# A hybrid decoder trunk: one weight combination of the Strassen MLP made by adding DMAs in place of VectorE, with the first two blocks' sums loaded ahead

## The chip, the cores and the metric

The kernel runs on one core of a Trainium2 chip. A core has four engines that compute: TensorE (PE, matmuls), VectorE (DVE), ScalarE (ACT) and GpSimd (POOL). SyncE (SP) issues transfers. Each engine works through its own list of instructions in order. The metric is the device time of one execution in microseconds; lower is better.

## The reference

The input is 512 tokens of width 1024 in float32. Two layers follow one another; each adds a mixer and then an MLP to the residual stream, and a final norm ends it.

```python
for i in range(DEPTH):                         # DEPTH = 2
    xn = rms_norm(x, norm_mix[i])
    mix = mla_mixer(xn, ...) if i % 2 == 0 else gla_mixer(xn, ...)
    x = x + mix
    x = x + sq_relu_mlp(rms_norm(x, norm_mlp[i]), mlp_w_up[i], mlp_w_down[i])
return rms_norm(x, final_norm)

def sq_relu_mlp(xn, w_up, w_down):             # w_up 1024 x 4096, w_down 4096 x 1024
    return jnp.square(jax.nn.relu(xn @ w_up)) @ w_down
```

The change lies in the two MLPs, in the norm that prepares their input, and in one small instruction at the start.

## The kernel before

**Precision.** A float32 matrix product is made of three products of the type fp32r. Each operand is split into a high part (ACT copies it into fp32r, line L112) and a low part (VectorE subtracts the high part from the value, L115). TensorE adds high by high, high by low and low by high. In the MLPs all weight pieces are split on the way in by `piece`, which names the parts `wh` and `wl` (three buffers each). Every matmul of an MLP is on line L818 (`matmuls`); it multiplies a 128x128 weight piece with 128x256 of the tokens.

**Strassen.** An MLP's products are made by the Winograd form of Strassen's scheme: seven block products in place of eight. In the up projection there are eight blocks b of 512 output columns. The 1024x512 weights of a block are cut into four quarters of 512x256, named 11, 12, 21 and 22 (in the code `a11`, `a12`, `a21`, `a22`, each 128x1024 in SBUF, 512 KB). The tokens are cut likewise; their combinations T1 to T4 are made once per MLP by `combine`. The seven steps of `up_block`, in the order in which the first two blocks run them:

- s0 and s1 load the quarters and multiply 11 by x11.
- s2 multiplies 12 (the product called "21").
- s5 makes S = 21 + 22 on VectorE (L904) and multiplies it by T1.
- s6 makes S - 11 (L919) and multiplies it by T2.
- s3 makes 12 - S (L925), multiplies it by x22 (the product "22"), and adds what belongs to it out of PSUM (L928).
- s7 makes 11 - 21 on VectorE (L932) and multiplies it by T3; L935 takes the sum out of PSUM.
- s4 multiplies 22 by T4, into the PSUM bank that L935 has read.

`finish` (L862, L863) applies relu, the norm's factor and the square. From block 2 on, s5 stands ahead of s2, there is no s0, and the steps alternate with those of a down projection.

The down projection works on pairs of blocks: `down_block(s)` for s = 0, 1, 2, with seven steps p1, p5, p6, p7, p2, p3, p4 on quarters of 512x512 (128x2048 in SBUF, 1 MB). p7 makes 11 - 21 of the weights on VectorE (L1004). The hidden values' combinations are on VectorE too (the `b11`, `b12`, `b21`, `b22` lines). Blocks 6 and 7 go through a plain product (`down`, `down_final`).

**Loads and buffers.** SP loads up quarters into five buffers of 512 KB (pool `up`, tag `raw`) and down quarters into three of 1 MB (pool `down_w`, tag `raw`). For blocks 0 and 1 the quarters 21 and 22 come as one 1 MB load each into a buffer of the down weights (`wide[b]`, L1116), because the up buffers still hold other data at that time. The third of these buffers takes the first down quarter, which is loaded directly behind (L950).

**Order.** A scheduler places the instructions of each engine; `tc.keep_in_program_order` holds some where they are written, `tc.issue_after` holds a load behind another.

## Time and profile before

| | us |
|---|---|
| median of three runs | 1080.58 |
| the runs | 1080.05, 1080.58, 1083.18 |
| the profiled execution | 1080.79 |
| its span in the trace | 1079.1 |

The profile is of one execution; 1.7 us of its time lie outside the span. Its page gives the busy time of each engine, a chain of work that ended last, and groups of instructions. The mean clock granted to TensorE was 0.997 of full speed. In the rows of the trace, a line's start and length are in microseconds, "x2" counts instructions that a row joins, and a bracket behind a row is the idle time ahead of it with what ended it. The products of the first MLP begin between 190 and 195 us, those of the second between 740 and 745.

### The profile page before, as it was taken

What the parts mean: (1) busy time and instruction counts of PE and PEld (TensorE: products, weight loads), DVE (VectorE), ACT (ScalarE), POOL (GpSimd) and SP (SyncE); (2) the same over time, 40 slices, a digit from 0 to 9 for tenths busy, and PEclk for the clock granted to TensorE, in tenths of its full rate; (3) what the DMA queues carried; (4) which work ended last, traced back from release to release, by engine and by line L of the source; (5) the groups of instructions that cost most, each with busy time, mean ns of one, the idle gap of its engine ahead of it and who ended that gap; (6) DMA issues with size and microseconds to landing.
All of it is one profiled execution on the core that took longest, in us unless ns stands there. A gap on an engine that the chain in (4) does not pass through costs nothing.

```text
span 1079.1 us, 17824 instructions
## 1 busy us (share of the span) xinstructions
PE 1058.9 (98%) x7322; PEld 977.1 (91%) x7322; DVE 890.0 (82%) x1210; ACT 640.2 (59%) x934; POOL 44.5 (4%) x78
## 2 busy tenths in 40 slices
PE   9999999989999999999999999999899999999997
PEld 7788888989999999988788888888899999999986
DVE  6789879999899899967565655678999899899865
ACT  6577655566667776644334735655565667766734
POOL 6400000000000000030000000000000000000000
PEclk9999999999999999999999999999999999999999
DMA  7312017143433433260222222234324423522412
GB/s 211 95 49 79 13 31 229 42 136 99 157 98 99 157 100 96 86 203 24 62 67 78 79 79 57 61 98 138 117 79 129 146 82 134 176 76 82 137 39 79
DMA packets 97969, 107.88 MB, mean 100 GB/s; under 512 B 8048, under 2 KB 72832, under 8 KB 97888
## 3 DMA queue, kind: packets, MB, share of 16 engines
q1 hardware_dynamic: 95872, 105.52, 31.1%
q8 instruction: 57, 0.93, 0.4%
q10 hardware_dynamic: 1952, 1.21, 0.4%
q0 software_dynamic: 64, 0.02, 0.1%
q14 instruction: 24, 0.20, 0.1%
HBM read 104.64 MB, written 2.10 MB: 99 GB/s over the span
## 4 chain that ended last, share of the span: by engine, by line
PE 84%; DVE 11%; issue 2%; ACT 2%; DMA 1%; SPq 0%; DVEq 0%; ACTq 0%
PE ps L818 39%; PE ps L120 12%; PE ps L122 12%; PE ps L121 12%; DVE wl L115 4%; PE ps L137 2%; PE ps L1371 2%; DMA wraw_ckv<-in_mla_w_in_dram 1%; DVE q L862 1%; DVE h L115 1%; DVE raw L925 1%; ACT wh L112 1%; DVE raw L932 1%; DVE raw L904 0%; PE ps L1408 0%
## 5 line engine op out<-in xcount | busy, mean ns | idle before, releaser
L112 ACT ACTIVATE wh<-raw 128x1024 fp32r<-128x1024 f32 x208 | 218.9, 1057 | 155.2 <-PE ps L818 84.3
L115 DVE TENSOR_TENSOR wl<-raw,wh 128x1024 fp32r<-128x1024 f32 x208 | 251.8, 1218 | 16.6 <-ACT wh L112 16.3
L818 PE MATMUL ps<-h,wh 128*128 128x256 f32 x1344 | 170.6, 279 | 0.0
L818 PEld LDWEIGHTS ps<-h,wh 128*128 128x128 f32 x1344 | 163.0, 188 | 0.0
L818 PE MATMUL ps<-h,wl 128*128 128x256 f32 x672 | 92.3, 279 | 2.1 <-DVE wl L115 2.1
L120 PE MATMUL ps<-set,wh 128*128 128x512 f32 x232 | 92.0, 397 | 0.7 <-ACT set L245 0.7
L121 PE MATMUL ps<-set,wh 128*128 128x512 f32 x232 | 91.2, 393 | 0.6 <-DVE set L246 0.6
L122 PE MATMUL ps<-set,wl 128*128 128x512 f32 x232 | 91.1, 393 | 0.0
L112 ACT ACTIVATE wh<-wraw 128x1024 fp32r<-128x1024 f32 x41 | 43.0, 1056 | 74.0 <-PE ps L122 41.5
L818 PEld LDWEIGHTS ps<-h,wl 128*128 128x128 f32 x672 | 84.5, 188 | 2.5 <-DVE wl L115 2.5
L863 ACT ACTIVATE q<-q 128x512 f32<-128x512 f32 x64 | 40.0, 629 | 46.4 <-DVE q L862 46.2
L120 PE MATMUL ps<-wh,set 128*128 128x512 f32 x144 | 59.7, 414 | 0.0
L115 DVE TENSOR_TENSOR wl<-wraw,wh 128x1024 fp32r<-128x1024 f32 x41 | 50.3, 1230 | 10.7 <-ACT wh L112 10.6
L115 DVE TENSOR_TENSOR h<-q,h 128x1024 fp32r<-128x1024 f32 x44 | 53.6, 1220 | 4.9 <-ACT h L112 4.9
L122 PE MATMUL ps<-wh,set 128*128 128x512 f32 x144 | 56.3, 391 | 0.0
L121 PE MATMUL ps<-wl,set 128*128 128x512 f32 x144 | 56.3, 391 | 0.0
L121 PEld LDWEIGHTS ps<-set,wh 128*128 128x128 f32 x232 | 44.0, 190 | 10.5 <-DVE set L246 1.3
L120 PEld LDWEIGHTS ps<-set,wh 128*128 128x128 f32 x232 | 43.9, 190 | 10.0 <-ACT set L245 1.0
L122 PEld LDWEIGHTS ps<-set,wl 128*128 128x128 f32 x232 | 44.0, 190 | 9.0
L112 ACT ACTIVATE h<-q 128x1024 fp32r<-128x1024 f32 x44 | 46.2, 1052 | 4.8 <-DVE q L988 2.1
L818 PE MATMUL ps<-T0h,wh 128*128 128x256 f32 x128 | 33.2, 283 | 7.1 <-DVE q L935 6.7
L120 PE MATMUL ps<-hh,wh 128*128 128x512 f32 x96 | 37.4, 389 | 0.0
(512 smaller groups left out, 2778.2 us busy)
## 6 DMA issues: line engine op xcount, KB each, us to landing
raw<-in_mlp_w_down_dram SPq DMA_DIRECT2D x38, 1024.0 KB, 5.2
raw<-in_mlp_w_up_dram SPq DMA_DIRECT2D x56, 512.0 KB, 3.9
wraw<-in_gla_w_in_dram SPq DMA_DIRECT2D x11, 1024.0 KB, 5.1
wraw<-in_mla_w_o_dram SPq DMA_DIRECT2D x8, 512.0 KB, 4.8
raw<-in_mlp_w_up_dram SPq DMA_DIRECT2D x4, 1024.0 KB, 8.0
wraw<-in_gla_w_o_dram SPq DMA_DIRECT2D x8, 512.0 KB, 4.9
xT<-in_x_dram SPq DMA_DIRECT2D x6, 256.0 KB, 7.5
wraw_qn<-in_mla_w_uq_dram SPq DMA_DIRECT2D x6, 256.0 KB, 3.4
```

The source lines that it names most:

```text
L112: raised.append(order(ACT.activation(hi, src, AF.Copy)))
L115: return lo_eng.tensor_tensor(lo, src, f(hi), ALU.subtract)
L120: PE.matmul(psum, wh, xh, start=start, stop=False, **kw)
L121: PE.matmul(psum, wh, xl, start=False, stop=False, **kw)
L122: PE.matmul(psum, wl, xh, start=False, stop=stop, **kw)
L137: PE.transpose(psum, src, ident[: src.shape[0], : src.shape[0]])
L818: return PE.matmul(p[:, m * TH : (m + 1) * TH], w[i][:, k - k0, m * P : (m + 1) * P], x[k][j], start=start, stop=stop, skip_group_check=True,)
L862: DVE.scalar_tensor_tensor(qs, c, 0.0, r, ALU.max, ALU.mult)
L863: ACT.activation(qs, qs, AF.Square)
L925: DVE.tensor_tensor(v["a12"], v["a12"], v["s"], ALU.subtract)
L932: DVE.tensor_tensor(v["a21"], v["a11"], v["a21"], ALU.subtract)
L1371: PE.matmul(p[:, t * 64 : (t + 1) * 64].rearrange("p (n c) -> p n c", c=m), k[:, sl], later, start=True, stop=True)
```

## The change

In each MLP VectorE no longer makes 11 - 21. A DMA on GpSimd's queue loads quarter 11 once more and adds it onto the buffer of quarter 21 (`accum_op=ALU.add`), which makes 11 + 21. To make the sum fit, the lower rows of the tokens are taken negated: `combine` gets the negated gains for two of its terms (`less`, a 128x16 tile, made once at the start by the new L1582), and further signs change in consequence: sums in place of differences at L919 and L925, the minimum in place of the maximum in `finish` for the second half, and signs of the hidden combinations. The down weights' 11 + 21 is made likewise (a 1 MB addition, L1019). In two places of the down block a scalar-and-tensor instruction takes the place of a plain one, of the same size (L1025, L1055).

For blocks 0 and 1 also S = 21 + 22 is made by a DMA: SP loads 21 into a third buffer, and GpSimd's queue adds 22 onto it. The six loads of 512 KB (two blocks times S's first half, 21 and 22) and the four additions now fill all three buffers of the down weights, so the first down quarter is no longer loaded ahead of them.

```diff
-            DVE.scalar_tensor_tensor(t2, u[:, first], g1, t3, ALU.mult, ALU.add)
+            DVE.scalar_tensor_tensor(t2, u[:, first], l1, t3, ALU.mult, ALU.subtract)
...
+            def fill_sums(s):
+                v["s"] = s
+                fill(s, 1, 0)
+                joint(s, 1, 1)
+                fill(wide[b][0], 1, 0)
+                joint(wide[b][0], 0, 0)
+                fill(wide[b][1], 1, 1)
+
+            def joint(t, half, trail):
+                POOL.dma_start(t, rows(half, trail), accum_op=ALU.add)
...
             def s5():
-                s = v["s"] = up.tile([P, KH, 256], F32, tag="raw", bufs=5, name=uname("raw"))
-                if "a12" not in v:
+                if "s" not in v:
+                    v["s"] = up.tile([P, KH, 256], F32, tag="raw", bufs=5, name=uname("raw"))
                     v["a12"] = unit(0, 1)
-                DVE.tensor_tensor(s, v["a21"], v["a22"], ALU.add)
+                    DVE.tensor_tensor(v["s"], v["a21"], v["a22"], ALU.add)
+                    joint(v["a21"], 0, 0)
+                s = v["s"]
...
             def s6():
-                DVE.tensor_tensor(v["s"], v["s"], v["a11"], ALU.subtract)
+                DVE.tensor_tensor(v["s"], v["s"], v["a11"], ALU.add)
             def s3():
-                DVE.tensor_tensor(v["a12"], v["a12"], v["s"], ALU.subtract)
+                DVE.tensor_tensor(v["a12"], v["a12"], v["s"], ALU.add)
             def s7():
-                DVE.tensor_tensor(v["a21"], v["a11"], v["a21"], ALU.subtract)
...
             def p5():
                 v["21"], v["S"] = quarter(1, 0), quarter(1, 1)
                 DVE.tensor_tensor(v["S"], v["21"], v["S"], ALU.add)
-                DVE.tensor_tensor(b11, b12, b11, ALU.subtract)
+                POOL.dma_start(v["21"], rows(0, 0), accum_op=ALU.add)
+                DVE.tensor_tensor(b11, b11, b12, ALU.subtract)
             def p6():
-                DVE.tensor_tensor(b11, b22, b11, ALU.subtract)
+                DVE.scalar_tensor_tensor(b11, b11, -1.0, b22, ALU.mult, ALU.subtract)
             def p7():
-                DVE.tensor_tensor(v["21"], v["11"], v["21"], ALU.subtract)
             def p4():
-                DVE.tensor_tensor(b21, b21, b11, ALU.subtract)
+                DVE.scalar_tensor_tensor(b21, b11, -1.0, b21, ALU.mult, ALU.subtract)
...
         for b in range(2):
-            t = wide[b] = wide_raw().rearrange("p a (b n) -> p (a b) n", b=2)
-            c0 = b * FB + 256
-            wide["last"] = SP.dma_start(t, w_up[:, c0 : c0 + 256].rearrange("(k p) n -> p k n", p=P))
+            wide[b] = halves(wide_raw())
+        for b, t in enumerate(halves(wide_raw())):
+            fills[b](t)
...
+    DVE.tensor_scalar(less, gains[:, GAIN_COL["mlp"] : GAIN_COL["mlp"] + 16], -1.0, None, ALU.mult)
```

In all 26 VectorE instructions go (16 of L932, 6 of L1004, 4 of L904), one small one comes, and 26 adding DMAs come (20 of 512 KB, 6 of 1 MB). The MLP's lines move down: L818 becomes L825, L862 becomes L889, L904 L931, L919 L948, L925 L954, L928 L957, L935 L963, L950 L981, L852 and L1116 L864.

The order of instructions changes as follows. On VectorE at the start of the first MLP, blocks 0 and 1, before (`raw_2248` and `raw_2250` hold 21 and 22 of the blocks, `raw_2390` and `raw_2548` their S):

```order
L925 TENSOR_TENSOR raw_2146<-raw_2146,raw_2390 128x1024
L904 TENSOR_TENSOR raw_2548<-raw_2250 128x1024
L115 TENSOR_TENSOR wl_2456<-raw_2146,wh_2455 128x1024
L115 TENSOR_TENSOR wl_2488<-raw_2248,wh_2487 128x1024
L932 TENSOR_TENSOR raw_2250<-raw_2156,raw_2250 128x1024
L928 TENSOR_TENSOR q_2253<-ps_2392,mt_2452 128x512
L115 TENSOR_TENSOR wl_2519<-raw_2248,wh_2518 128x1024
L862 SCALAR_TENSOR_TENSOR q_2253<-q_2253,rstd_2327 128x512
L115 TENSOR_TENSOR wl_2552<-raw_2548,wh_2551 128x1024
L935 TENSOR_TENSOR q_2253<-ps_2279,mt_2421 128x512
L919 TENSOR_TENSOR raw_2548<-raw_2548,raw_2156 128x1024
```

and now, in the same place (`raw_2251` holds both S, `raw_2249` 21 and 22 of block 0):

```order
L954 TENSOR_TENSOR raw_2147<-raw_2147,raw_2251 128x1024
L115 TENSOR_TENSOR wl_2433<-raw_2251,wh_2432 128x1024
L115 TENSOR_TENSOR wl_2464<-raw_2147,wh_2463 128x1024
L115 TENSOR_TENSOR wl_2495<-raw_2249,wh_2494 128x1024
L115 TENSOR_TENSOR wl_2526<-raw_2249,wh_2525 128x1024
L957 TENSOR_TENSOR q_2263<-ps_2400,mt_2460 128x512
L115 TENSOR_TENSOR wl_2557<-raw_2251,wh_2556 128x1024
L889 SCALAR_TENSOR_TENSOR q_2263<-q_2263,rstd_2337 128x512
L948 TENSOR_TENSOR raw_2251<-raw_2251,raw_2157 128x1024
L963 TENSOR_TENSOR q_2263<-ps_2289,mt_2429 128x512
L954 TENSOR_TENSOR raw_2159<-raw_2159,raw_2251 128x1024
```

L904 and L932 are gone; block 1's S sum with 11 (L948) now stands ahead of L963, where its counterpart L919 stood behind L935.

On VectorE around the last down block of the first MLP, before (`raw_5150` is the down quarter 12):

```order
L115 TENSOR_TENSOR wl_5121<-raw_4988,wh_5120 128x1024
L925 TENSOR_TENSOR raw_4989<-raw_4989,raw_4988 128x1024
L932 TENSOR_TENSOR raw_4953<-raw_4951,raw_4953 128x1024
L1008 TENSOR_TENSOR xT<-ps_5028,xT 128x4x256
L1009 TENSOR_TENSOR sum_0_2243<-ps_5028,sum_0_2243 128x1024
L862 SCALAR_TENSOR_TENSOR q_4949<-ps_4957,rstd_2327 128x512
L1010 TENSOR_TENSOR xT<-xT,sum_0_2243 128x4x256
L115 TENSOR_TENSOR wl_5158<-raw_5150,wh_5157 128x1024
```

and now:

```order
L115 TENSOR_TENSOR wl_5126<-raw_4993,wh_5125 128x1024
L954 TENSOR_TENSOR raw_4994<-raw_4994,raw_4993 128x1024
L1055 SCALAR_TENSOR_TENSOR q_4041<-q_3615,q_4041 128x1024
L1039 TENSOR_TENSOR xT<-ps_5033,xT 128x4x256
L1040 TENSOR_TENSOR sum_0_2244<-ps_5033,sum_0_2244 128x1024
L889 SCALAR_TENSOR_TENSOR q_4954<-ps_4962,rstd_2337 128x512
L1041 TENSOR_TENSOR xT<-xT,sum_0_2244 128x4x256
L115 TENSOR_TENSOR wl_5163<-raw_5155,wh_5162 128x1024
```

L932's place is taken by L1055, the hidden combination of p4, which stood further on.

On SP at the start of the first MLP, before:

```order
L852 DMA raw_2158<-in_mlp_w_up_dram 128x4x256
L1116 DMA raw_2248<-in_mlp_w_up_dram 128x8x256
L1116 DMA raw_2250<-in_mlp_w_up_dram 128x8x256
L950 DMA raw_2782<-in_mlp_w_down_dram 128x4x512
L852 DMA raw_2710<-in_mlp_w_up_dram 128x4x256
```

and now, on SP,

```order
L864 DMA raw_2159<-in_mlp_w_up_dram 128x4x256
L864 DMA raw_2251<-in_mlp_w_up_dram 128x4x256
L864 DMA raw_2249<-in_mlp_w_up_dram 128x4x256 x2
L864 DMA raw_2251<-in_mlp_w_up_dram 128x4x256
L864 DMA raw_2250<-in_mlp_w_up_dram 128x4x256 x2
L864 DMA raw_2714<-in_mlp_w_up_dram 128x4x256
L864 DMA raw_2716<-in_mlp_w_up_dram 128x4x256
L864 DMA raw_2718<-in_mlp_w_up_dram 128x4x256
L981 DMA raw_2787<-in_mlp_w_down_dram 128x4x512
```

and on POOL, where nothing stood between the first mixer and here:

```order
L878 DMA raw_2251<-in_mlp_w_up_dram 128x4x256
L878 DMA raw_2249<-in_mlp_w_up_dram 128x4x256
L878 DMA raw_2251<-in_mlp_w_up_dram 128x4x256
L878 DMA raw_2250<-in_mlp_w_up_dram 128x4x256
L878 DMA raw_2716<-in_mlp_w_up_dram 128x4x256
L1019 DMA raw_2911<-in_mlp_w_down_dram 128x4x512
```

The first down quarter (L950, now L981) moves behind three up loads. On TensorE the order is the same as before.

## The prediction

> **What bounds the kernel now.** I read the page's busy row first, then its chain, then the table of waits by engine.

> ```profile
> span 1079.1 us, 17824 instructions
> PE 1058.9 (98%) x7322; PEld 977.1 (91%) x7322; DVE 890.0 (82%) x1210; ACT 640.2 (59%) x934; POOL 44.5 (4%) x78
> PE 84%; DVE 11%; issue 2%; ACT 2%; DMA 1%; SPq 0%; DVEq 0%; ACTq 0%
> PE ps L818 <- DVE q L935: 6.7, 4, 2.0
> PE ps L818 <- DVE wl L115: 2.4, 3, 1.1
> PE ps L818 <- ACT wh L112: 1.4, 3, 0.5
> ```

> TensorE is busy for 98% of the span, so an edit that only empties VectorE is worth what TensorE waited for it, and no more. The last three rows (total us, times, longest us) are all of those waits at the MLPs' matmuls: 6.7 + 2.4 + 1.4 = 10.5 us. In the timeline of TensorE they are ten places; the bracket gives the wait and what ended it.

> ```profile
> 209.33 0.39 PE L818 MATMUL ps<-x4h,wh 128*128 128x256 f32 x1 [0.47 <-ACT wh L112]
> 217.02 0.36 PE L818 MATMUL ps<-T0h,wh 128*128 128x256 f32 x1 [1.77 <-DVE q L935]
> 232.66 0.39 PE L818 MATMUL ps<-T0h,wh 128*128 128x256 f32 x1 [1.53 <-DVE q L935]
> 445.84 0.86 PE L818 MATMUL ps<-h,wl 128*128 128x256 f32 x5 [1.07 <-DVE wl L115]
> 759.21 0.38 PE L818 MATMUL ps<-T0h,wh 128*128 128x256 f32 x1 [0.41 <-ACT wh L112]
> 762.69 0.38 PE L818 MATMUL ps<-x4h,wh 128*128 128x256 f32 x1 [0.47 <-ACT wh L112]
> 770.39 0.36 PE L818 MATMUL ps<-T0h,wh 128*128 128x256 f32 x1 [1.97 <-DVE q L935]
> 787.26 0.39 PE L818 MATMUL ps<-T0h,wh 128*128 128x256 f32 x1 [1.40 <-DVE q L935]
> 908.78 0.39 PE L818 MATMUL ps<-T0h,wl 128*128 128x256 f32 x1 [0.26 <-DVE wl L115]
> 1001.40 0.86 PE L818 MATMUL ps<-h,wl 128*128 128x256 f32 x5 [1.06 <-DVE wl L115]
> ```

> Seven of the ten lie in the first two blocks of an MLP (209 to 233, 759 to 788), two at the last down block (445.84, 1001.40), one in a later block. Everywhere else VectorE is nearly full too, yet TensorE does not wait. The windows show it, and one loss of another kind (busy us and count of PE, PEld, DVE, ACT, POOL; then the granted clock, DMA share, GB/s):

> ```profile
> 340.00:360.00 20.00, 20.00 (x176) 20.00 (x175) 19.86 (x20) 13.47 (x17) 0.00 (x0) 1.00 0.23 76
> 771.00:775.00 4.00, 4.00 (x23) 4.00 (x23) 3.25 (x4) 2.64 (x3) 0.00 (x0) 0.57 0.83 273
> 775.00:779.00 4.00, 4.00 (x37) 4.00 (x37) 3.95 (x4) 3.24 (x5) 0.00 (x0) 1.00 0.46 134
> ```

> In the steady stretch VectorE works 19.86 us of 20 and TensorE 20.00: time freed there is worth nothing today. Behind the longest wait (770.39) the clock was granted at 0.57, and 23 matmuls went through in 4 us where 37 go at full clock: (37 - 23) / 37 x 4 = 1.5 us lost. No such row stands behind the 1.77 us wait at 217.02.

> **The change, part by part.**

> *What leaves VectorE.* Groups of VectorE (count | busy us, mean ns of one):

> ```profile
> L932 DVE TENSOR_TENSOR raw<-raw,raw 128x1024 f32<-128x1024 f32 x16 | 19.5, 1219 | 0.1
> L1004 DVE TENSOR_TENSOR raw<-raw,raw 128x2048 f32<-128x2048 f32 x6 | 13.7, 2283 | 0.0
> L904 DVE TENSOR_TENSOR raw<-raw 128x1024 f32<-128x1024 f32 x4 | 4.9, 1219 | 0.0
> ```

> All three go: 26 instructions, 19.5 + 13.7 + 4.9 = 38.1 us. If TensorE waited for VectorE all the time, this would be the gain; the ten rows above cap it at 10.5 + 1.5 = 12.0 us. What is left is to ask, place by place, how much of each wait the freed time reaches.

> *The three waits for the high weight part (1.4 us; 209.33, 759.21, 762.69).* ACT's cast is behind a VectorE sum of the first two blocks: two L904 and two L932 stood among them. With four instructions of about 1.1 us fewer ahead of these casts, nothing of a wait of 0.5 us is left. I take 1.4 of 1.4. What comes next there is the sum L948 (formerly L919), which stands earlier by the same amount.

> *The four waits before T4 (6.7 us).* TensorE's T4 product reuses the bank that L935 empties. VectorE before the first of them, and before the second (with T3's first matmul ahead):

> ```profile
> 212.26 0.28 PE L818 MATMUL ps<-T0h,wh 128*128 128x256 f32 x1
> ...
> 212.72 0.68 DVE L928 TENSOR_TENSOR q<-ps,mt 128x512 f32<-128x512 f32 x1
> 213.32 1.22 DVE L115 TENSOR_TENSOR wl<-raw,wh 128x1024 fp32r<-128x1024 f32 x1
> 214.45 0.69 DVE L862 SCALAR_TENSOR_TENSOR q<-q,rstd 128x512 f32<-128x512 f32 x1
> 215.05 1.22 DVE L115 TENSOR_TENSOR wl<-raw,wh 128x1024 fp32r<-128x1024 f32 x1
> 216.19 0.68 DVE L935 TENSOR_TENSOR q<-ps,mt 128x512 f32<-128x512 f32 x1
> ...
> 224.92 1.22 DVE L932 TENSOR_TENSOR raw<-raw,raw 128x1024 f32<-128x1024 f32 x1
> 229.59 0.69 DVE L928 TENSOR_TENSOR q<-ps,mt 128x512 f32<-128x512 f32 x1
> 231.93 0.68 DVE L935 TENSOR_TENSOR q<-ps,mt 128x512 f32<-128x512 f32 x1
> ```

> Block 0: in the changed order five instructions stand in the same place: L957, L115, L889, L948, L963. They are of the same shapes (the 1.22 us sum L948 where an L115 of 1.22 stood), so the chain from the first of them to T4 stays 217.02 - 212.72 = 4.30 us. L957 needs the bank of "22". That product's last matmul starts one matmul (0.11 us) before T3's first at 212.26, and at 0.28 each it ends at 212.43. L928 started 0.29 us after that, because L932 was still running; without it the chain starts some 0.26 us sooner. The wait becomes 1.5 us in each MLP: 0.27 saved of 1.77, 0.47 of 1.97.

> Block 1: the sum between them is in block 0 only, and L932 (224.92) no longer pushes L928, so L963 is there before T3 ends. T3 ends at 232.66 - 1.53 = 231.13. From there it takes L963's 0.68 us, 0.04 us before and 0.05 to 0.15 behind it (216.19 + 0.68 to 217.02 is 0.15, 231.93 + 0.68 to 232.66 is 0.05): a wait of 0.85 us stays whatever VectorE does. Saved: 0.68 and 0.55. Together 6.7 becomes 4.7 or 4.8: I take 1.9.

> *The waits for the low weight part (2.4 us).* The rows around the last down block of the first MLP, and the sum ahead of the 908.78 wait:

> ```profile
> 415.67 1.23 DVE L115 TENSOR_TENSOR h<-q,h 128x1024 fp32r<-128x1024 f32 x1 [0.64 <-ACT h L112]
> 416.81 0.68 DVE L928 TENSOR_TENSOR q<-ps,mt 128x512 f32<-128x512 f32 x1
> 444.57 2.35 DVE L115 TENSOR_TENSOR wl<-raw,wh 128x1024 fp32r<-128x1024 f32 x2
> 904.64 1.23 DVE L932 TENSOR_TENSOR raw<-raw,raw 128x1024 f32<-128x1024 f32 x1
> ```

> At 908.78 the L932 two rows ahead of the awaited cast goes: 1.23 us against a wait of 0.26. At 445.84 the case is less clear: in the changed order a new L1055 (128x1024, scalar and tensor) stands where an L932 stood, so inside this stretch VectorE has as much as before. But its backlog begins at 416.81, behind rows that L1004 and the 0.64 us idle of the row at 415.67 had made late; those sit more than a microsecond sooner, and VectorE runs without a pause to 444.57. The wait is 1.07. I take all 2.4 as gained; the ends are 0.26 (only 908.78) and 2.4.

> *The clock (1.5 us).* The half-clock stretch came behind a 1.97 us wait and not behind 1.77. The forecast has 1.5 there, below both, so I take the 1.5 us as saved; ends 0 and 1.5. [...]

> *New instructions on VectorE.* L1025 and L1055 as scalar-and-tensor of 128x1024 have no row. 128x512 ones have: 0.69 (214.45) against 0.68 for the plain one (212.72), so I take them equal to those they replace; ends: equal, and 0.02 us more each (under 0.3 us in all). One small 128x16 at the start: between nothing and 0.7 us (a 128x512 at 0.68); I take 0, since it is 1/32 of that. Changed signs and min for max cost nothing: the same instruction in the same place.

> *The accumulating DMAs.* 26 of them, on GpSimd's queue, which had small work only (44.5 us busy in the page); no row of before shows one that adds. The nearest rows (KB, median us from issue to landing), the first issues, and the first cast that needs a sum:

> ```profile
> raw<-in_mlp_w_up_dram SPq DMA_DIRECT2D x56, 512.0 KB, 3.9
> raw<-in_mlp_w_up_dram SPq DMA_DIRECT2D x4, 1024.0 KB, 8.0
> invf<-in_inv_freq_dram POOLq DMA_DIRECT2D x1, 16.0 KB, 6.9
> ...
> 177.35 1.00 SPq L1116 DMA_DIRECT2D raw<-in_mlp_w_up_dram  x2
> 199.46 1.06 ACT L112 ACTIVATE wh<-raw 128x1024 fp32r<-128x1024 f32 x1 [0.48 <-DVE raw L904]
> ```

> Low end: adding costs no more than loading. Two 1 MB loads land in 8.0 us together; six fills and four additions are 5.2 MB, so about 20 us: all done at 197. High end: each addition takes a GpSimd landing and a plain load one after the other, 6.9 + 3.9 = 10.8 us, and they run one by one behind a first fill (177.35 + 3.9 = 181.3): 192, 203, 214, 225. Needed are S of block 0 by 199 (cast at 199.46) and S of block 1 by some 211: the subtraction behind its 1.06 us cast is the L115 at 213.32 in the chain above, ahead of L963. For the T3 weights I estimate 207 and 222, some five us ahead of their products (212.26; 231.13 - 2.9). The low end makes all four; the high end is 3 us late for the two latter. I take the low end's side, nearer to the 512 KB load, 3.9 to 6 us each, at no cost. In later blocks the addition is issued behind the sum S and has 18 to 28 VectorE rows, some 20 us, until its cast; in down blocks 31 rows: either price is covered. The 18 MB more of traffic runs beside a DMA share of 0.23 (steady window). If that cover goes, T3 waits.

> *Fills and the down load.* SP issues six loads of 512 KB for two of 1 MB, and the first down quarter goes behind them and three up loads; it is needed tens of microseconds later. Cost nothing; the cover is the same low DMA share.

> *Sum:* 1.4 + 1.9 + 2.4 + 1.5 = 7.2 us. The profiled execution took 1080.79 us, 1.7 outside its span, 0.2 over the median of the three runs (1080.58). 1080.79 - 7.2 = 1073.6; I say 1073.5.

> **Rivals.**

> *A, slower: the additions come late.* If they pass one at a time at the high price, S of block 1 lands 3 us late; VectorE's in-order queue then holds its cast, L963 behind it, and T4, in both MLPs: 6 us of the 7.2 given back, 1079.5. The kernel gets slower by over 0.3% (3.2 us, about what a measurement can tell) from (7.2 + 3.2) / 2 = 5.2 us late, which is (211 + 5.2 - 181.3) / 3 = 11.6 us each, and each further microsecond per addition costs 6 us: at 13 us, 1088. For it: they share one queue, and 16 KB there took 6.9 us. Against: most of that must be a start-up, which overlaps between queued transfers.

> *B, the freed time is just idle.* Only the waits for the high part go, and the small 0.26: VectorE then waits for TensorE at its in-order reads of banks and arrives at T4 and at the last down block as before. Gain 1.7 to 3: 1078 to 1079. For it: two of the largest waits keep L948 or L1055 in the chain.

> *C, the clock drops again,* or stays as it was: 1075.1, still faster. A drop in the first MLP too: 1076.6. For it: the same kind of wait stays at 1.5 us.

> *D, all ten waits go:* 12.0 us, 1068.8. Against: the evacuation of 0.85 us cannot go.

> **How the numbers follow.** Forecast with or without C (gain 4.5 to 9): 0.55. A gain above 9 (D in part): 0.05. A part of it, 3.3 to 4.5: 0.12. B, or A at about the high price (within 0.3%): 0.16. A beyond that: 0.12. So faster 0.72, same 0.16, slower 0.12. Range: up to 1079.5 (B and the high price of A in), from 1071.0 (the 1.5 us waits down to 0.85 each and some more); below and above are left about 0.05 and 0.13. The forecast's own range is 1071.5 to 1076.5.

> **What the changed profile would show.** Right: three waits for L112 gone; waits for L963 four times, near 1.5 and 0.85 us; no wait for L115 at the last down block; 1.00 clock behind T4 of block 0 in both MLPs; VectorE about 37 us less busy. Wrong: a wait of VectorE or ACT on an addition, with TensorE behind it; 512 KB additions that take over 11 us from issue to landing; or VectorE idle ahead of L963 while TensorE waits.

## The result and the profile after

The changed kernel took 1075.14 us (median of 4, 1073.5 to 1075.3) where the kernel before took 1080.89 on the same chip (median of 4): a ratio of 0.994, with a 95% interval of 0.9922 to 0.9958. In a second set on one chip it was 1074.37 for 1083.26, 0.9919 (0.9904 to 0.9934). Forecast were 1073.5 us, a range of 1071.0 to 1079.5, and faster. The profiled execution took 1075.1 us with a span of 1073.4.

The page's first rows and its DMA issues, and the table of TensorE's waits (total us, times, longest):

```profile
span 1073.4 us, 17924 instructions
PE 1057.3 (98%) x7322; PEld 975.7 (91%) x7322; DVE 858.0 (80%) x1185; ACT 640.5 (60%) x934; POOL 76.1 (7%) x104
raw<-in_mlp_w_up_dram POOLq DMA_DIRECT2D x20, 512.0 KB, 6.4
raw<-in_mlp_w_down_dram POOLq DMA_DIRECT2D x6, 1024.0 KB, 9.2
PE ps L825 <- DVE q L963: 4.8, 4, 1.5
PE ps L120 <- ACT set L245: 1.6, 2, 0.9
PE ps L121 <- DVE set L246: 1.1, 1, 1.1
```

VectorE is 32 us less busy, the span 5.7 us shorter. Of the three rows with 10.5 us at the MLPs' matmuls, one is left with 4.8. The waits for the high and the low part are gone. The four that remain, in TensorE's timeline:

```profile
218.12 0.38 PE L825 MATMUL ps<-T0h,wh 128*128 128x256 f32 x1 [1.50 <-DVE q L963]
233.30 0.39 PE L825 MATMUL ps<-T0h,wh 128*128 128x256 f32 x1 [0.78 <-DVE q L963]
768.62 0.39 PE L825 MATMUL ps<-T0h,wh 128*128 128x256 f32 x1 [1.50 <-DVE q L963]
783.50 0.38 PE L825 MATMUL ps<-T0h,wh 128*128 128x256 f32 x1 [0.99 <-DVE q L963]
```

10.5 - 4.8 = 5.7 us of waits. In the windows (columns as in the prediction), the stretch behind the T4 wait of the second MLP is at full clock now, the steady stretch is unchanged for TensorE, and one at the start is not at full clock:

```profile
340.00:360.00 20.00, 20.00 (x176) 20.00 (x175) 19.51 (x18) 12.86 (x16) 1.28 (x1) 1.00 0.44 113
768.70:772.70 4.00, 4.00 (x35) 4.00 (x36) 3.76 (x5) 2.33 (x4) 0.00 (x0) 1.00 0.53 140
16.00:20.00 4.00, 4.00 (x12) 3.17 (x11) 2.51 (x4) 2.00 (x2) 3.66 (x6) 0.57 0.43 125
```

The kernel before passed that stretch of the start at full clock:

```profile
16.00:20.00 4.00, 4.00 (x19) 3.31 (x18) 2.46 (x4) 2.38 (x3) 3.66 (x7) 1.00 0.40 115
```

Lining up the 7322 matmuls of both traces one by one, the changed kernel is 1.9 us behind at the 58th matmul (19.5 us), and from there to the last waits at 996 us it wins 7.6 us: 5.7 of waits, 1.5 of clock, the rest in steps of 0.1 us. The start took 1.9 of them back, which leaves 5.7.

### The profile page after: what moved, and what is told of

The parts are those of the page before. It is cut to its first block, busy times and chain, and to the rows that moved or that the text cites. A ratio compares the mean times of both kernels' runs of the same rounds, so it can differ in the third digit from the quotient of the medians.

```text
span 1073.4 us, 17924 instructions
## 1 busy us (share of the span) xinstructions
PE 1057.3 (98%) x7322; PEld 975.7 (91%) x7322; DVE 858.0 (80%) x1185; ACT 640.5 (60%) x934; POOL 76.1 (7%) x104
## 5 line engine op out<-in xcount | busy, mean ns | idle before, releaser
L112 ACT ACTIVATE wh<-raw 128x1024 fp32r<-128x1024 f32 x208 | 219.4, 1058 | 152.9 <-PE ps L825 100.0
L115 DVE TENSOR_TENSOR wl<-raw,wh 128x1024 fp32r<-128x1024 f32 x208 | 251.5, 1219 | 26.8 <-ACT wh L112 26.3
L825 PE MATMUL ps<-h,wh 128*128 128x256 f32 x1344 | 170.5, 279 | 0.0
L825 PEld LDWEIGHTS ps<-h,wh 128*128 128x128 f32 x1344 | 162.9, 188 | 0.0
L825 PE MATMUL ps<-h,wl 128*128 128x256 f32 x672 | 92.2, 279 | 0.2
L112 ACT ACTIVATE wh<-wraw 128x1024 fp32r<-128x1024 f32 x41 | 43.0, 1056 | 73.9 <-PE ps L122 41.6
L825 PEld LDWEIGHTS ps<-h,wl 128*128 128x128 f32 x672 | 84.5, 188 | 0.6 <-DVE wl L115 0.6
L878 POOL DMA_DIRECT2D raw<-in_mlp_w_up_dram x20 | 25.8, 1290 | 707.3 <-DVE raw L931 313.9
L890 ACT ACTIVATE q<-q 128x512 f32<-128x512 f32 x64 | 40.2, 628 | 46.7 <-DVE q L889 46.3
L115 DVE TENSOR_TENSOR h<-q,h 128x1024 fp32r<-128x1024 f32 x44 | 53.7, 1222 | 9.9 <-ACT h L112 9.8
L115 DVE TENSOR_TENSOR wl<-wraw,wh 128x1024 fp32r<-128x1024 f32 x41 | 50.2, 1227 | 10.8 <-ACT wh L112 10.7
L112 ACT ACTIVATE h<-q 128x1024 fp32r<-128x1024 f32 x44 | 46.1, 1050 | 0.6 <-DVE q L1020 0.6
L825 PE MATMUL ps<-T0h,wh 128*128 128x256 f32 x128 | 33.0, 281 | 4.8 <-DVE q L963 4.8
## 6 DMA issues: line engine op xcount, KB each, us to landing
raw<-in_mlp_w_down_dram SPq DMA_DIRECT2D x38, 1024.0 KB, 5.2
raw<-in_mlp_w_up_dram SPq DMA_DIRECT2D x68, 512.0 KB, 5.5
wraw<-in_gla_w_in_dram SPq DMA_DIRECT2D x11, 1024.0 KB, 5.1
raw<-in_mlp_w_up_dram POOLq DMA_DIRECT2D x20, 512.0 KB, 6.4
raw<-in_mlp_w_down_dram POOLq DMA_DIRECT2D x6, 1024.0 KB, 9.2
wraw<-in_mla_w_o_dram SPq DMA_DIRECT2D x8, 512.0 KB, 4.8
wraw<-in_gla_w_o_dram SPq DMA_DIRECT2D x8, 512.0 KB, 4.8
```

Source lines behind the costliest of these rows:

```text
L112: raised.append(order(ACT.activation(hi, src, AF.Copy)))
L115: return lo_eng.tensor_tensor(lo, src, f(hi), ALU.subtract)
L825: return PE.matmul(p[:, m * TH : (m + 1) * TH], w[i][:, k - k0, m * P : (m + 1) * P], x[k][j], start=start, stop=stop, skip_group_check=True,)
L878: POOL.dma_start(t, rows(half, trail), accum_op=ALU.add)
L890: ACT.activation(qs, qs, AF.Square)
```

## The experiments

All are written from the changed kernel. "Waits" are TensorE's at the MLPs' matmuls, in us, in the one execution of each kernel that was profiled. Of the half clock it is said where the profile has it at an MLP's matmuls.

| | waits before T4 | for the high part | for the low part | sum |
|---|---|---|---|---|
| before | 6.7 | 1.4 | 2.4 | 10.5 |
| changed | 4.8 | 0 | 0 | 4.8 |
| changed, second profile | 5.0 | 0 | 0 | 5.0 |
| blocks 0, 1 only | 7.1 | 0 | 2.4 | 9.5 |
| blocks 0, 1, 2 only | 5.1 | 0 | 2.7 | 7.8 |
| later blocks only | 7.0 | 1.3 | 0 | 8.3 |
| up weights only | 5.2 | 0 | 3.3 | 8.5 |
| no additions | 5.0 | 0 | 0 | 5.0 |
| sum held behind L963 | 4.7 | 0 | 0 | 4.7 |
| both held behind | 3.1 | 0 | 0 | 3.1 |

The two profiles of the changed kernel differ by 0.2 us, so a difference of that size between kernels says nothing.

**Blocks 0 and 1 only.** From block 2 on and in the down blocks VectorE adds 11 to 21 itself:

```diff
             def s7():
+                if b > 1:
+                    DVE.tensor_tensor(v["a21"], v["a11"], v["a21"], ALU.add)
...
             def p7():
+                DVE.tensor_tensor(v["21"], v["11"], v["21"], ALU.add)
```

(with the additions on GpSimd's queue of these blocks taken out)

> Additions by DMA only in the first two blocks of each MLP; from block 2 on and in the down blocks VectorE adds 11 to 21 itself again (18 of the 26 instructions are back). Theory 1 (what counts are the waits in the first two blocks and, by the freed rows right ahead of them, at three later places): the waits for L112 stay gone, the four waits before T4 stay at 1.5 and 0.85 us, the half-clock stretch behind T4 stays away, but TensorE waits again for the low part at three places, about 2.4 us: some 2.4 us slower than the changed kernel, about 3.5 us faster than before. Rival (VectorE's load as such is what counts, 26 us of it is back): two thirds of the gain goes, 1079 us. Rival 2 (the later additions cost hidden time): as fast as the changed kernel or faster.

Measured: 1080.12 us, ratio 0.998 (0.9971 to 0.9989), 5.0 to 5.8 us slower than the changed kernel where theory 1 had 2.4. The waits for the high part are gone and those for the low part back, as expected; but the waits before T4 of block 1 are 2.05 us, longer than before, and all waits together are 4.7 us longer than in the changed kernel. The timeline of TensorE:

```profile
216.85 0.39 PE L825 MATMUL ps<-T0h,wh 128*128 128x256 f32 x1 [1.50 <-DVE q L964]
232.79 0.39 PE L825 MATMUL ps<-T0h,wh 128*128 128x256 f32 x1 [2.05 <-DVE q L964]
768.85 0.38 PE L825 MATMUL ps<-T0h,wh 128*128 128x256 f32 x1 [1.50 <-DVE q L964]
784.79 0.39 PE L825 MATMUL ps<-T0h,wh 128*128 128x256 f32 x1 [2.05 <-DVE q L964]
```

and VectorE ahead of the second of them (L961 is block 2's sum, back; L956 is the changed kernel's L957):

```profile
227.44 1.22 DVE L961 TENSOR_TENSOR raw<-raw,raw 128x1024 f32<-128x1024 f32 x1
228.57 0.69 DVE L956 TENSOR_TENSOR q<-ps,mt 128x512 f32<-128x512 f32 x1
...
230.91 1.22 DVE L115 TENSOR_TENSOR h<-q,h 128x1024 fp32r<-128x1024 f32 x1
232.05 0.69 DVE L964 TENSOR_TENSOR q<-ps,mt 128x512 f32<-128x512 f32 x1
```

Block 2's sum stands ahead of block 1's chain and pushes the low part of a hidden operand into it. So the two parts of the change are not worth the sum of what each is worth alone. In its total the rival's 1079 us came nearer than theory 1; the places of the waits and the next two runs speak against it.

**Blocks 0, 1 and 2 only** tests that: two VectorE instructions less.

```diff
+                    if b == 2:
                         joint(v["a21"], 0, 0)
...
+                if b > 2:
+                    DVE.tensor_tensor(v["a21"], v["a11"], v["a21"], ALU.add)
```

> Adding DMAs in blocks 0, 1 and 2 only; from block 3 on and in the down blocks VectorE adds. Against the run with the first two blocks only, two VectorE instructions less (block 2's 11 + 21 in each MLP). Theory 1 (the instruction ahead of block 1's L957 is what made T4 of block 1 wait 2.05 us): that wait falls to 0.78 to 0.99 us in both MLPs, 2.1 to 2.5 us less for 2.4 us of VectorE; the 2.4 us of waits for the low part stay. Rival: the wait depends on VectorE's load over the whole stretch and falls by a part only.

1077.98 us in one run. Both waits before T4 of block 1 fell, to 0.99 and 1.00 us: 2.1 us for two instructions of 1.2 us, which is what theory 1 asked for. The low part still cost 2.7 us.

**Later blocks only.** Blocks 0 and 1 as before the change (two 1 MB loads, S and 11 + 21 on VectorE).

```diff
-        for b, t in enumerate(halves(wide_raw())):
-            fills[b](t)
+            wide["last"] = SP.dma_start(joined(t), w_up[:, c0 : c0 + 256]...)
...
             def s7():
+                if b < 2:
+                    DVE.tensor_tensor(v["a21"], v["a11"], v["a21"], ALU.add)
```

> The first two blocks as before (two 1 MB loads, S and 11 + 21 on VectorE), the DMA additions from block 2 on and in the down blocks. Theory 1: only the waits for the low part (2.4 us) go, the waits before T4 and for L112 are back as before (6.7 and 1.4 us), and with them the chance of a half-clock stretch of 1.5 us: 1077 to 1079 us. Rival (load as such): two thirds of the gain stays, 1077 or less, and the T4 waits shrink too. The two rivals and theory 1 differ most in the rows of TensorE's waits, not in the total.

Measured: 1079.57 us, 0.9976 (0.9967 to 0.9984), 0.6 us above the expected band; 2.2 us of waits gone (all of the low part's), the four before T4 at 7.0. The half clock came here behind T4 of the first MLP, behind a wait of 1.77 us (windows of this run):

```profile
219.00:223.00 4.00, 3.89 (x22) 3.92 (x23) 3.96 (x4) 2.40 (x3) 0.00 (x0) 0.63 0.91 312
```

The rival that counts VectorE's load as such loses in both: 28 us of it back (12 sums of 1.22 us and 6 of 2.28) or 10 (8 of 1.22) leave nearly the same time.

**Up weights only.** The six 1 MB additions go back to VectorE, the up ones stay.

```diff
-                POOL.dma_start(v["21"], rows(0, 0), accum_op=ALU.add)
...
             def p7():
+                DVE.tensor_tensor(v["21"], v["11"], v["21"], ALU.add)
```

> Adding DMAs for all up weights; the down weights' 11 + 21 on VectorE again (6 instructions of 2.28 us). The question is what removed the 1.07 us waits for the low part at the last down blocks. As the prediction has it (L1004 made VectorE late ahead of the backlog there): both waits of about 1.07 us are back, the waits before T4 and the 0.26 us one are not; 2.1 us slower than the changed kernel at the same clock. Rival (the up sums counted): the waits stay away and the six instructions cost nothing.

1077.04 us in one run. The waits at the last down blocks are back, and longer than before:

```profile
445.20 1.21 PE L825 MATMUL ps<-h,wl 128*128 128x256 f32 x8 [1.55 <-DVE wl L115]
997.66 1.21 PE L825 MATMUL ps<-h,wl 128*128 128x256 f32 x8 [1.71 <-DVE wl L115]
```

The 0.26 us one is not. So it is taking out the down weights' sum that removed the 1.07 us waits, which the prediction said with less certainty than the rest.

**No additions.** All 26 adding DMAs left out, nothing in their place.

```diff
             def joint(t, half, trail):
-                POOL.dma_start(t, rows(half, trail), accum_op=ALU.add)
+                pass
```

> All adding DMAs left out, with nothing in their place (weights of T3 are 21 alone, S of the first two blocks also). Theory 1 (the additions are hidden everywhere): same time as the changed kernel within 0.5 us, same waits. Rival A (they cost, by contention or late landings): faster by the cost, 1 us or more, with a wait of the changed kernel that is gone here.

1073.79 us, waits of 1.50, 0.99, 1.50, 0.99, as in the second profile of the changed kernel. The additions cost nothing that can be seen in the trace: lined up with the first profile of the changed kernel, the matmuls end 0.2 us earlier (spans 1073.2 and 1073.4, both with a half-clock stretch at the start). The median time is 0.6 to 1.4 us lower, in runs whose mean clock is higher (0.9980 for 0.9974); so the times alone don't rule out a cost of up to about a microsecond.

**Two doses of additions.** First, every addition but three in each MLP made twice, one behind the other:

```diff
                 joint(s, 1, 1)
+                if b == 1:
+                    joint(s, 1, 1)
...
                     joint(v["a21"], 0, 0)
+                    joint(v["a21"], 0, 0)
...
                 POOL.dma_start(v["21"], rows(0, 0), accum_op=ALU.add)
+                POOL.dma_start(v["21"], rows(0, 0), accum_op=ALU.add)
```

> Dose for rival A, inside the slack: in each MLP the addition onto S of block 1, and every later addition (blocks 2 to 7, and the down weights'), is made twice, one behind the other (the weights then hold 11 once too often, or 22 in S). In the changed kernel the addition to S of block 1 lands at 202 us and the cast that needs it runs at 212.9; later additions land after 6 us (512 KB) or 9 us (1 MB). A second one costs about 6 to 8 us more. Theory 1 (additions are hidden with about 10 us to spare): same time within 0.5 us and the same waits. Rival A (they were just in time, or the doubled traffic slows other loads): slower, with new waits for L112 or L115.

1074.63 us, the waits of the changed kernel to the tenth:

```profile
PE ps L825 <- DVE q L966: 4.8, 4, 1.5
```

Then the first blocks' four, twice each:

```diff
             def joint(t, half, trail):
                 POOL.dma_start(t, rows(half, trail), accum_op=ALU.add)
+                if b < 2:
+                    POOL.dma_start(t, rows(half, trail), accum_op=ALU.add)
```

> The dose beyond the slack: all four additions of blocks 0 and 1 are made twice in each MLP (S with 22 twice, T3's weight with 11 twice); the later ones as in the changed kernel. On GpSimd's queue the second waits for the first to land. By 8 us for each second addition, S of block 0 lands near 204 (its cast was at 201), S of block 1 near 215 (cast at 213): waits of 2 to 4 us at T1 and up to 3 us at T4 of block 0 in each MLP, 4 to 14 us slower in all. If the time doesn't move, the additions run far quicker than they land in the changed kernel; if it moves by over 30 us, they pass one at a time at 10 us or more each, as rival A had it.

1078.74 us, with waits that the changed kernel does not have:

```profile
205.87 0.39 PE L825 MATMUL ps<-T0h,wh 128*128 128x256 f32 x1 [0.37 <-ACT wh L112]
209.82 0.39 PE L825 MATMUL ps<-T0h,wh 128*128 128x256 f32 x1 [0.94 <-ACT wh L112]
758.15 0.38 PE L825 MATMUL ps<-T0h,wh 128*128 128x256 f32 x1 [0.80 <-ACT wh L112]
761.82 0.39 PE L825 MATMUL ps<-T0h,wh 128*128 128x256 f32 x1 [0.58 <-ACT wh L112]
```

2.7 us of waits at T1 and T2; lined up with the changed kernel's, its matmuls are 3.4 us behind, less than the 4 to 14 expected, since T4 did not wait for S of block 1, which landed at 212.9, ahead of its cast at 214.69. Nor do the waits at T1 and T2 show what a late addition costs. S of block 0 had landed at 202.2, but its cast stands in this kernel behind another ACT instruction that waits for VectorE:

```profile
204.24 0.63 ACT L892 ACTIVATE q<-q 128x512 f32<-128x512 f32 x1 [3.00 <-DVE q L891]
204.78 1.04 ACT L112 ACTIVATE wh<-raw 128x1024 fp32r<-128x1024 f32 x1
```

In the changed kernel the cast (200.95) stands ahead of that instruction (L890, 205.00). So these waits hold the new order of ACT as well as the landing, which came 1.3 us behind the time of the cast in the changed kernel, and the run doesn't separate the two.

**The sum held behind L963.** The prediction left 1.5 us before T4 of block 0, because block 1's L948 stands ahead of L963.

```diff
+                with tc.issue_after(wide["out"].ins) if b == 1 else nullcontext():
                     DVE.tensor_tensor(v["s"], v["s"], v["a11"], ALU.add)
```

(`wide["out"]` is the instruction of L963 in the block ahead)

> The changed kernel with the sum S + 11 of block 1 (L948, 1.14 us) held behind the read of the T3 sum out of PSUM (L963) of block 0, as it stood in the kernel before. Theory 1: the wait before T4 of block 0 falls from 1.5 to about 0.85 us in both MLPs (L963 cannot start before T3 has ended), 1.2 to 1.3 us faster than the changed kernel, and no new wait at T2 of block 1, which comes 11 us later. Rival B (in-order reads make the wait come back elsewhere): L948 late makes T2 of block 1 wait, and the total does not move.

1073.94 us, 0.9924 (0.9911 to 0.9936), and waits of 4.7 us for 4.8: no gain. Block 0's fell to 0.78, block 1's rose to 1.60 and 1.50: rival B, in small, and at T4 of block 1, not at T2. The scheduler put the low part of p5's hidden operand into the free place, ahead of block 1's L963 (here L964):

```profile
228.53 0.68 DVE L889 SCALAR_TENSOR_TENSOR q<-q,rstd 128x512 f32<-128x512 f32 x1
229.13 1.22 DVE L115 TENSOR_TENSOR h<-q,h 128x1024 fp32r<-128x1024 f32 x1
230.26 0.68 DVE L964 TENSOR_TENSOR q<-ps,mt 128x512 f32<-128x512 f32 x1
```

**Both held behind.** The same, and that low part too:

```diff
+                with tc.issue_after(wide["out"].ins) if s == 0 and n == 5 else nullcontext():
+                    DVE.tensor_tensor(h[:, 1], t, f(h[:, 0]), ALU.subtract)
```

> The changed kernel with two VectorE instructions held back: the sum S + 11 of block 1 behind the read of the T3 sum (L963) of block 0, and the low part of p5's hidden operand (an L115 of 1.14 us, which the scheduler puts ahead of block 1's L963 once the sum is moved) behind L963 of block 1. Theory 1: both waits before T4 are 0.78 us in both MLPs, where the changed kernel has 1.50 and 0.78 to 0.99: 3.1 us in all for 4.8, 1.4 to 1.7 us faster than the changed kernel at the same clock. Rival B: the held instruction is late for p5 and the wait comes back there, no gain.

```profile
PE ps L825 <- DVE q L964: 3.1, 4, 0.8
```

Four waits of 0.78 us, and 1072.88 us in the set in which the changed kernel took 1074.37: 1.5 us less as expected, though the four runs of each overlap (1072.3 to 1074.16 and 1073.04 to 1075.13). In the trace, lined up with the changed kernel's, the T4 places of block 0 give 0.7 us each. It has the lowest median of all versions tried, 0.9905 (0.9888 to 0.9921) of before.

**The changed kernel once more.**

> The changed kernel once more, on the same chip as the others of this set. Expected: about 1074 to 1075 us, waits before T4 of 1.50, 0.78 to 0.99, 1.50 and 0.99 us, no others of L112 or L115 at the MLPs' matmuls. What differs is the place of half-clock stretches, at the start above all: if the new small VectorE instruction there caused the slower start of the first profile (2.0 us behind the kernel before by 19.5 us), this profile shows it again; if it is chance, the start takes another course.

The waits were 1.50, 0.99, 1.50 and 0.99 us, as expected. Its start went at full clock in the same stretch (19 matmuls in 4 us), with the same small VectorE instruction in it:

```profile
16.00:20.00 4.00, 4.00 (x19) 3.26 (x18) 2.51 (x4) 2.19 (x3) 3.58 (x8) 1.00 0.46 132
```

So the new instruction alone does not slow the start: the same kernel starts with and without the half clock. Of the thirteen profiles with this instruction seven have a half-clock stretch between 14 and 20 us, and the one profile of the kernel before has none; whether the instruction makes it likelier is not shown. A stretch at the end, behind the last matmul, is in all fourteen profiles and slows no matmul.

**A longer wait before T4.** Further additions on VectorE into a buffer that nobody reads any more, three of 128x1024, 128x512 and 128x256 in one kernel, three of 128x1024 in the other:

```diff
+                i = wide["mid"]
+                for w in (KH, 2, 1) if b == 0 else ():
+                    with tc.issue_after(i.ins):
+                        i = DVE.tensor_tensor(v["a12"][:, :w], v["a12"][:, :w], v["a11"][:, :w], ALU.add)
+                with tc.issue_after(i.ins):
                     DVE.tensor_tensor(c, pairs(v["b2"]), pairs(v["p5"]), ALU.add)
```

> The changed kernel with three further VectorE additions into a buffer that is no longer read (128x1024, 128x512, 128x256) ahead of block 0's L963, to make the wait before T4 longer: by 0.9 us, to about 2.4 us, in both MLPs. The question is the half clock, which in the profiles so far came behind some waits of 1.77 to 1.98 us, not behind others of 1.60 to 2.05, and never behind 1.50. Theory 1 (a wait of some 2 us is enough when it falls well into a window of activity; longer makes it likelier): half clock behind one or both T4 waits, mean granted clock about 0.995 to 0.996 over the runs, 3 to 5 us slower than the changed kernel for 1.9 us of waits. [...]

> The same with three additions of 128x1024: the wait before T4 of block 0 becomes 1.50 + 2.28 = about 3.8 us in both MLPs, longer than the 3.4 us for which a half-clock stretch lasts. Theory 1: half clock behind both waits in nearly every run, 1.5 us each, 7 to 8 us slower than the changed kernel for 4.6 us of waits, clock about 0.995. [...]

1079.80 and 1082.07 us, mean clock over ten runs each 0.9953 and 0.9942. The waits were 2.43 and 3.77 us in both MLPs (a row of the shorter and one of the longer):

```profile
217.34 0.39 PE L825 MATMUL ps<-T0h,wh 128*128 128x256 f32 x1 [2.43 <-DVE q L968]
774.49 0.58 PE L825 MATMUL ps<-T0h,wh 128*128 128x256 f32 x1 [3.77 <-DVE q L968]
```

The windows behind all four are at half clock (the first two rows of the shorter, the last two of the longer):

```profile
218.00:222.00 4.00, 4.00 (x23) 4.00 (x23) 3.29 (x4) 2.63 (x3) 0.00 (x0) 0.57 0.99 319
771.00:775.00 4.00, 3.99 (x20) 3.99 (x21) 3.96 (x4) 1.90 (x3) 0.00 (x0) 0.57 0.86 277
...
220.50:224.50 4.00, 4.00 (x21) 4.00 (x22) 3.91 (x4) 1.85 (x3) 0.00 (x0) 0.57 0.88 280
774.50:780.50 6.00, 6.00 (x28) 6.00 (x29) 4.42 (x5) 2.63 (x3) 0.00 (x0) 0.51 0.89 274
```

The changed kernel did not run in this set. Against its medians of the other two (1075.14 and 1074.37) the shorter is 4.7 to 5.4 us slower, the longer 6.9 to 7.7; by the ratios to the kernel before (0.9973 and 0.9995 for 0.994 and 0.9919) it is 3.6 to 5.8 and 5.9 to 8.2. Their waits are 8.1 and 9.3 us in all, 3.3 and 4.5 more than 4.8 (in the shorter, block 1's T4 wait grew to 1.6 too, which was not expected). What the medians leave, about 1.4 to 2.1 and 2.4 to 3.2 us, agrees roughly with an estimate from the mean clock: 0.0021 and 0.0032 below the changed kernel's 0.9974, of some 1078 us, are 2.3 and 3.4. That is theory 1.

## Why the prediction was right, point by point

*The high part, 1.4 us:* all three waits gone. *The waits before T4:* forecast 1.5 and 0.85 us, measured 1.50 twice, 0.78 and 0.99; 1.9 of 6.7 saved, as forecast. In the 0.78 us L963 takes 0.69 and starts 0.03 behind T3's end (232.52 to 232.55), where the forecast had 0.04. That block 1's part of it hangs on block 2's sum (L932 at 224.92 in the prediction) is shown by the runs with two and three blocks. *The low part, 2.4 us:* all gone. The run on the up weights shows the down weights' sum as the cause at the last down blocks, and the way is the prediction's: the backlog that began at 416.81 begins at 416.49 now, while TensorE there is 0.63 us later than before, so it has a start of 0.95 us where the prediction said more than a microsecond. The 0.26 us wait stays away in that run and is back (0.27) in the one with the first two blocks alone, so it needs an up sum, as forecast.

*The clock, 1.5 us:* the half-clock stretch at T4 is gone, as forecast. What the sum left out is the rest of the clock: it held the start fixed, and the profiled execution of the changed kernel met a half-clock stretch there, which is why it is 1.6 us above 1073.5. The profiled execution of before had just one such stretch at T4; of the four waits of 1.77 to 1.98 us that the two profiles with the old order of the first blocks have, two were followed by one. Over the runs the term has about its size: the mean granted clock of 54 runs of the kernel before is 0.9961, of 8 of the changed kernel 0.9974, and 0.0013 of some 1078 us is 1.4 us. This is an estimate, since the mean clock counts the stretch at the end too. The ratio is lower in the second set (0.9919) mainly because the kernel before took longer there (1083.26 for 1080.89); the cause of that is open.

The half clock followed waits of 1.77, 1.97 and 2.43 us. It lasted about 3.4 us behind those (3.413 in the clock record of the kernel before, from 771.185 to 774.598), and about twice that behind the 3.77 us wait in the second MLP, where 28 matmuls took 6 us. In the profiles, 2 of 6 waits of 1.77 to 2.05 us at the MLPs' matmuls were followed by it, none of more than twenty of 1.50 to 1.71, and all four of 2.43 and 3.77.

The traces show more of the waits near 2 us. In theory 1 of the longer waits the "window of activity" was the author's assumption, with no row behind it; what the profiles have is this. In each of the nine profiles that have two or more half-clock stretches, these begin a whole number of 3.413 us apart (303.786 us = 89 x 3.4133 in the kernel before, 1054.718 us = 309 x 3.4133 in the changed one). With the profiles cut into cells of that length, with the begin of a stretch as the edge of a cell, the cells ahead of these stretches were idle for about half or more. The first two rows are the 1.97 us wait of the kernel before, the next two the 1.77 us wait of the run with the later blocks only, then its 1.98 us wait, which is shared by two cells, and the start of the changed kernel:

```profile
767.77:771.18 3.41, 1.44 (x13) 1.27 (x12) 3.41 (x5) 0.63 (x1) 0.00 (x0) 1.00 0.56 163
771.18:774.59 3.41, 3.41 (x19) 3.41 (x18) 3.07 (x4) 2.60 (x3) 0.00 (x0) 0.50 0.91 294
...
216.64:220.05 3.41, 1.64 (x14) 1.46 (x14) 3.41 (x5) 0.63 (x1) 0.00 (x0) 1.00 0.57 194
220.05:223.46 3.41, 3.41 (x19) 3.41 (x18) 2.92 (x4) 2.63 (x3) 0.00 (x0) 0.50 0.83 267
769.60:773.01 3.41, 1.83 (x17) 1.63 (x15) 3.41 (x5) 0.63 (x1) 0.00 (x0) 1.00 0.37 76
773.01:776.42 3.41, 3.01 (x25) 3.04 (x26) 3.41 (x5) 1.75 (x3) 0.00 (x0) 1.00 0.91 322
...
12.83:16.24 3.41, 1.59 (x6) 1.11 (x7) 3.29 (x4) 3.06 (x6) 3.22 (x5) 1.00 0.98 308
16.24:19.65 3.41, 3.41 (x10) 2.67 (x9) 1.92 (x3) 2.00 (x2) 3.07 (x6) 0.50 0.46 133
```

*The additions, nothing:* right, and shown by leaving them out. The addition to S of block 1 was issued at 189.75 and landed 12.4 us later, at 202, the cast that needs it ran at 212.89; the forecast had it needed by 211 and done between 197 and 214. The least cover is that of S of block 0: landed at 195.3, cast at 200.95. One sign that the prediction named as wrong did come, 512 KB additions of over 11 us: six of the eight in the first two blocks took 12.1 to 13.5 us, more than rival A's high price of 10.8 for each. They cost nothing since they were under way together and landed 2.6 to 4.1 us apart in the first MLP, so the sign was badly chosen: the time of one addition says little, the time of landing against the cast counts. *Freed VectorE time as such, nothing:* right; the steady window is 20.00 of 20 as before. *L1025 and L1055 as dear as plain ones:* right; in the groups of VectorE (busy us, mean ns) they stand at 1218 and 1217 where the plain one next to them has 1216.

```profile
L1025 DVE SCALAR_TENSOR_TENSOR q<-q,q 128x1024 f32<-128x1024 f32 x6 | 7.3, 1218 | 0.0
L1055 DVE SCALAR_TENSOR_TENSOR q<-q,q 128x1024 f32<-128x1024 f32 x6 | 7.3, 1217 | 0.0
L1020 DVE TENSOR_TENSOR q<-q,q 128x1024 f32<-128x1024 f32 x6 | 7.3, 1216 | 0.0
```

VectorE's busy time fell by 32 us where about 37 were forecast. The lengths of its rows together did fall by 37.5 us (965.5 to 928.0); but neighbouring rows overlap by some 0.08 us, the busy time counts an overlap once, and with fewer rows back to back 5.5 us of overlap went too.

Rival A was not seen: the additions overlapped (the first two were issued 1.4 us apart, at 185.56 and 186.9, and landed 9.8 and 12.4 us later), and even with all four of the first blocks doubled the waits were not shown to be theirs. What share of such a time is a start-up, as the prediction argued, no run shows. Rival A's sum for 13 us each is off: three additions of 2.2 us more than 10.8 make S of block 1 some 9 us late in each MLP, about 1092 us and not 1088. B came true only where an instruction was moved. D stopped at the 0.78 us that the evacuation takes: with both instructions held behind, the read (L964) itself waits for TensorE, and 0.78 is what stays. C (1075.1) met the number for another reason, a stretch at the start and not at T4, and that the measured 1075.1 is C's figure to the tenth is luck.

## What to carry to other kernels

Where one engine is at 98%, list the places where it waits and ask of each which instructions stand ahead of the awaited one in its queue; 38 us of work removed from another engine was worth the 5.7 us of waits that this reached, and two instructions of 1.2 us at the right place were worth 2.1 us of waits. Parts of such a change did not add up here, since one part moved the place at which the other counts: 1.0 us of waits went with blocks 0 and 1 alone, 2.2 with the later blocks alone, 5.7 with both. Price a wait of about 2 us and more on TensorE at its length plus the half clock that may follow: in these profiles it followed 2 of 6 waits of 1.77 to 2.05 us and all four of 2.43 and 3.77, and a stretch of 3.41 us cost 1.5 us; what decides among waits near 2 us was not shown in full.

## What the runs showed of the hardware that was not expected

The packets of the adding DMAs took twice the time of a load's for each MB. On the page of the changed kernel (packets, MB, share of 16 engines):

```profile
q1 hardware_dynamic: 98048, 107.62, 31.6%
q0 software_dynamic: 13792, 16.80, 10.1%
```

0.60% for each MB on GpSimd's queue, 0.29% on the other. 512 KB landed a median 6.4 us after issue, against 3.9 for a load in the kernel before; at the start of each MLP it took 9.8 to 13.5. The loads beside the additions landed later too, which the waits don't show: plain 512 KB loads of up weights landed a median 5.5 us after issue in the changed kernel (5.2 in its second profile), 4.6 in the run on the up weights, which has the 1 MB additions left out, and 6.1 where most additions were made twice.
